# A two-layer diffusion backbone: the norm's sum of squares in two sets of matmuls

## The chip, the cores and the metric

The kernel runs on one core of a Trainium2 chip. The metric is the device time in microseconds (us) of one execution, as a median of three runs. The core's engines work side by side, each through its own queue in order: TensorE (PE in the profile; its weight loads are PEld), VectorE (DVE), ScalarE (ACT), GpSimd (POOL), and SyncE (SP), which here only issues DMAs. TensorE's clock has two levels, 1.2 and 2.4 GHz; the profile gives the granted clock as a share of the full one.

## The reference

640 tokens (128 of context, 512 latent) of width 1024 go through two layers. A layer norms x, projects it into the inputs of three mixers (differential attention, a bidirectional state-space scan, neighbourhood attention), merges their outputs, projects once more and adds the result to x. A last norm gives y. What the change touches is the norm alone:

```
def _rmsnorm(x, g):
    xf = x.astype(jnp.float32)
    y = xf * lax.rsqrt(jnp.mean(xf * xf, axis=-1, keepdims=True) + EPS)
    return (y * g.astype(jnp.float32)).astype(x.dtype)
```

## The kernel before, in words

The activations lie transposed: x is 8 tiles of 128 features by 640 tokens, worked on in two halves of 320 tokens. Nearly all matmuls are in `feat` (the matmul is line 175): an output tile of 128 features by 320 tokens takes 8 k-tiles, and each k-tile three products of high and low parts in the reduced format fp32r, 24 in all. Weights come by DMA into `raw`; ACT rounds them to `hi` (L150) and DVE makes the rest `lo` (L151).

`rms_x` (line 323) makes the norm's factor for one half. The sum over features is a sum over partitions and over the 8 tiles. ACT squares each tile (L328, L331), DVE adds the squares into `acc` (L332, seven additions), and three matmuls of one column each, with 128 tokens of `acc` as weights and a column of ones as moving data, put the sum of each token into a partition of `ms` (L338). All of this is in full fp32, and a matmul in fp32 shows as two records of the weight load and two of the matmul, so the three show as six. DVE scales and adds EPS (L339), POOL raises to the power -0.5 (L340, `r`). Then the factor must lie along the free axis again: DVE multiplies three pieces of the identity with columns of `r` (L346, `d`), and one matmul of ones with `d` (L348, `rb`, 320 columns, fp32) copies it to all partitions. The three pieces start at tokens 0, 128 and 192 of the half, so that the last repeats 64 tokens.

`rms_x` is called six times: for the two halves at the start (lines 1110 and 1113), for the two halves between the layers (through `norm`, line 1192) and for the two halves at the end (line 1194). Between the layers and at the end it follows `out_proj` (line 1051), whose eight tiles m are added to x by DVE (L1057); as each x tile comes out, its square and its addition can go. At the end DVE multiplies x by `rb` and `final_g` (L1196, eight operations per half) and SP sends each tile out. Nothing comes after the second half but this.

Who runs first on an engine is settled before the run: the program is built under a scheduler with a simulated timeline, which takes on each engine the ready instruction that comes first in the program. On the chip each engine keeps that order. `bank()` hands out PSUM tiles from a pool of three, and `warm` (line 204) shows a use that the kernel has already: matmuls that nobody reads.

Of the kernel before, what the change touches and what calls it, by code (L numbers as in the profile page):

```python
# [9 lines left out]
F32 = mybir.dt.float32  # L10
F32R = mybir.dt.float32r
AF = mybir.ActivationFunctionType
ALU = mybir.AluOpType
# [6 lines left out]
EPS = 1e-6  # L20
# [104 lines left out]
class Net:  # L125
# [106 lines left out]
    def load_first(self):  # L232
        nc, a, c = self.nc, self.a, self.const
        self.sm = {}
        self.load(["cc"])
        cc = self.sm["cc"]
        self.mhalf = c.tile([128, 8], F32, name="mhalf")
        nc.vector.memset(self.mhalf, -0.5)
        self.sc = c.tile([128, 8, 32], F32, name="sc")
        nc.vector.memset(self.sc, 0.0)  # L240
        th = c.tile([128, 8, 2], F32, name="cth")
        nc.scalar.activation(th, cc, AF.Tanh, scale=0.5)
        nc.vector.tensor_scalar(out=th, in0=th, scalar1=0.5, scalar2=0.5, op0=ALU.mult, op1=ALU.add)
        nc.vector.tensor_tensor(out=self.sc[:, :, 0:2], in0=th, in1=cc, op=ALU.mult)
# [75 lines left out]
        out.append(g)  # L320


    def rms_x(self, x, half, pool, pp):
        nc = self.nc
        h0 = half * 320
        h = slice(h0, h0 + 320)
        acc = pool.tile([128, 320], F32, tag="acc", name="acc", bufs=2)
        nc.scalar.activation(acc, x[0][:, h], AF.Square)  # L328
        for k in range(1, 8):
            sq = pool.tile([128, 320], F32, tag="sq", name="sq", bufs=2)  # L330
            nc.scalar.activation(sq, x[k][:, h], AF.Square)  # L331
            nc.vector.tensor_tensor(out=acc, in0=acc, in1=sq, op=ALU.add)  # L332
        at = (0, 128, 192)
        ps = pp.tile([128, 512], F32, tag="ms", name="ms", bufs=1)
        v = pool.tile([128, 3], F32, tag="v", name="v", bufs=2)
        r = pool.tile([128, 3], F32, tag="r", name="r", bufs=2)
        for i, c in enumerate(at):
            nc.tensor.matmul(ps[:, i:i + 1], lhsT=acc[:, c:c + 128], rhs=self.ones[:, 0:1], start=True, stop=True)  # L338
        nc.vector.tensor_scalar(out=v, in0=ps[:, 0:3], scalar1=1.0 / 1024, scalar2=EPS, op0=ALU.mult, op1=ALU.add)  # L339
        nc.gpsimd.tensor_tensor(out=r, in0=v, in1=self.mhalf[:, 0:3], op=ALU.pow)  # L340
        self.r = r
        rb = pp.tile([128, 512], F32, tag="rb", name="rb", bufs=2)[:, 0:320]
        d = pool.tile([128, 320], F32, tag="d", name="d", bufs=2)
        for i, c in enumerate(at):
            own = slice(0, 128) if i < 2 else slice(64, 128)
            nc.vector.tensor_scalar(out=d[:, c + own.start:c + 128], in0=self.ident[:, own], scalar1=r[:, i:i + 1], scalar2=None,  # L346
                                    op0=ALU.mult)
        nc.tensor.matmul(rb, lhsT=self.ones, rhs=d, start=True, stop=True)  # L348
        return rb

    def norm(self, l, x, half, ss, p, pp):
# [710 lines left out]
    def build(self):  # L1062
        nc, tc, a, o = self.nc, self.tc, self.a, self.o
        with ExitStack() as es:
# [20 lines left out]
            with self.pool("x0") as xp, self.pool("aw0", bufs=9) as wp, self.pool("ps_a0", space=PSUM) as pp:  # L1085
                xa = xp.tile([128, 8, NT], F32, name="x")
                x = [xa[:, k, :] for k in range(8)]
# [13 lines left out]
                with self.pool("norm") as np_:  # L1101
# [8 lines left out]
                    rb = [self.rms_x(x, 0, np_, pp)]  # L1110
# [22 lines left out]
            for l in range(DEPTH):  # L1133
                with ExitStack() as ph:
                    with self.pool("dv") as vp:
# [4 lines left out]
                        pp = ph.enter_context(self.pool("ps_c", space=PSUM))  # L1140
                        v = self.diff_v(l, 0, vp)
                        self.logits(l, 1, range(8))
                        self.logits(l, 0, L1)
                        with self.pool("diff") as p, self.pool("ps_d", space=PSUM) as ps:
# [3 lines left out]
                            for h in range(4):  # L1148
# [7 lines left out]
                                if h == 1:  # L1156
                                    v = self.diff_v(l, 1, vp)
                                d = self.diff_norm(att, cp, pp)
# [20 lines left out]
                with self.pool("tail") as tp, self.pool("more", bufs=3) as more, self.pool("ps_x", space=PSUM) as pp:  # L1179
                    mg = [tuple(tp.tile([128, NT], F32R, name=f"mg{s}{k}") for s in "hl") for k in range(8)]  # L1180
                    self.merges(l, 2, range(4), accd, mg=mg, spilled=range(8), more=more)
                    with self.pool("x") as xp, self.pool("norm") as np_:
                        x = [xp.tile([128, NT], F32, name=f"x{k}") for k in range(8)]
                        for k in range(8):
                            self.dma(x[k], src[k])
                        for half in range(2):
                            h = slice(half * 320, half * 320 + 320)
                            self.out_proj(l, mg, x, gate[0], half)
                            if l + 1 < DEPTH:
                                for k in range(8):  # L1190
                                    self.dma(xd[k][:, h], x[k][:, h])
                                self.norm(l + 1, x, half, nxt, np_, pp)
                            else:
                                rb = self.rms_x(x, half, np_, pp)
                                for k in range(8):
                                    nc.vector.scalar_tensor_tensor(out=x[k][:, h], in0=x[k][:, h],  # L1196
                                                                   scalar=self.sm["final_g"][:, k:k + 1], in1=rb,
                                                                   op0=ALU.mult, op1=ALU.mult)
                                    self.dma(o["y"][k][:, h], x[k][:, h])
                        src = xd  # L1200
# [25 lines left out]
```

## Time and profile before

| what | us |
|---|---|
| median of 3 runs (lowest, highest) | 1624.2 (1621.79, 1625.91) |
| the profiled execution | 1621.39 |
| its span, first to last instruction | 1619.5 |
| PE busy in the span | 1580.0 (98%) |
| DVE busy | 1069.5 (66%) |
| ACT busy | 771.9 (48%) |
| POOL busy | 159.4 (10%) |

The profiled execution is 1.89 us longer than its span, and 2.8 us below the median of the runs. Matmuls are pipelined: the duration of a record runs from its start to its modelled end, and the next may start long before that. What a row of matmuls costs is read from start to start. Mean granted clock of TensorE over the span: 0.994.

### The profile page before, as it was taken

Reading aid. Unit: us, or ns where it says so; the run is one execution under the profiler, and the core shown is the slowest. Engines: PE = TensorE matmul, PEld = TensorE weight load, DVE = VectorE, ACT = ScalarE, POOL = GpSimd, SP = SyncE. Lnnn points to the kernel's source line nnn. Section 1 sums busy time; section 2 is a strip of 40 time slices with the busy share of each in tenths; the row PEclk is TensorE's granted clock in tenths of the full one; section 3 lists DMA queues with packets and bytes.
Section 4 is the critical chain, followed back from the end, with each engine's and each line's share of the span. In section 5 each row is a group of like instructions: output and inputs, shape, how many; then the busy total and the mean of one; then the engine's idle time right before and its main releaser. Section 6 shows DMA issues by size and latency. Waiting matters only on the chain.

```text
span 1619.5 us, 29029 instructions
## 1 busy us (share of the span) xinstructions
PE 1580.0 (98%) x11311; PEld 1503.4 (93%) x11311; DVE 1069.5 (66%) x2290; ACT 771.9 (48%) x1778; POOL 159.4 (10%) x182
## 2 busy tenths in 40 slices
PE   7999999999999999999999999999999999999997
PEld 4999899999989999999989989999999899999996
DVE  5766678667546666666777667766565575577565
ACT  4545654344445454453455465434444454554332
POOL 2003412011000000000000252201010000000000
PEclk9999999999999999999999999999999999999998
DMA  9563234421233434437553222352222343344643
GB/s 338 203 249 110 94 101 145 141 73 57 85 116 104 136 111 127 150 108 250 187 174 116 86 91 89 117 189 77 67 87 80 120 130 93 111 133 152 218 156 129
DMA packets 81672, 214.62 MB, mean 133 GB/s; under 512 B 9728, under 2 KB 25664, under 8 KB 80512
## 3 DMA queue, kind: packets, MB, share of 16 engines
q1 hardware_dynamic: 80624, 211.46, 40.1%
q8 instruction: 89, 1.46, 0.4%
q0 software_dynamic: 480, 0.88, 0.1%
q10 hardware_dynamic: 432, 0.43, 0.1%
q14 instruction: 47, 0.39, 0.1%
HBM read 170.27 MB, written 34.08 MB: 126 GB/s over the span
## 4 chain that ended last, share of the span: by engine, by line
PE 88%; DMA 4%; DVE 3%; issue 2%; ACT 2%; POOL 0%; SPq 0%; POOLq 0%; DVEq 0%; ACTq 0%
PE mm L175 61%; PE mm L187 7%; PE s L959 2%; PE o L983 2%; PE o L541 2%; PE t L975 2%; PE s L526 2%; PE t L533 1%; PE g L788 1%; DMA aw<-in_w_ada 1%; PE y L801 1%; DMA raw<-in_w_feat 1%; PE y L266 1%; PE s L522 1%; DMA raw<-in_w_out 1%
## 5 line engine op out<-in xcount | busy, mean ns | idle before, releaser
L175 PE MATMUL mm<-hh,hi 128*128 128x320 f32 x1856 | 575.6, 311 | 7.0 <-ACT hh L365 2.2
L175 PE MATMUL mm<-hl,hi 128*128 128x320 f32 x1856 | 578.5, 312 | 1.7 <-DVE hl L366 1.7
L175 PE MATMUL mm<-hh,lo 128*128 128x320 f32 x1856 | 574.4, 310 | 0.7 <-DVE lo L151 0.7
L175 PEld LDWEIGHTS mm<-hh,hi 128*128 128x128 f32 x1856 | 349.0, 188 | 16.4 <-issue 3.7
L175 PEld LDWEIGHTS mm<-hl,hi 128*128 128x128 f32 x1856 | 349.0, 188 | 7.9 <-issue 2.7
L175 PEld LDWEIGHTS mm<-hh,lo 128*128 128x128 f32 x1856 | 349.5, 188 | 5.9 <-issue 3.4
L151 DVE TENSOR_TENSOR lo<-raw,hi 128x1024 fp32r<-128x1024 f32 (+2 forms) x194 | 232.6, 1200 | 94.3 <-ACT hi L150 88.6
L150 ACT ACTIVATE hi<-raw 128x1024 fp32r<-128x1024 f32 (+2 forms) x194 | 200.1, 1033 | 176.5 <-PE mm L175 120.4
L175 PE MATMUL mm<-yh,hi 128*128 128x320 f32 x384 | 118.6, 310 | 3.4 <-ACT yh L385 3.4
L175 PE MATMUL mm<-yl,hi 128*128 128x320 f32 x384 | 119.2, 310 | 0.3 <-DVE yl L386 0.2
L175 PE MATMUL mm<-yh,lo 128*128 128x320 f32 x384 | 118.1, 308 | 0.0
L187 PE MATMUL mm<-hi,hh 128*128 128x264 f32 (+1 forms) x320 | 90.7, 284 | 1.8 <-DVE vl L406 1.7
L187 PE MATMUL mm<-lo,hh 128*128 128x264 f32 (+1 forms) x320 | 91.1, 285 | 0.0
L187 PE MATMUL mm<-hi,hl 128*128 128x264 f32 (+1 forms) x320 | 90.3, 283 | 0.0
L535 ACT ACTIVATE ph<-t 128x384 fp32r<-128x384 f32 x64 | 31.4, 490 | 121.5 <-PE t L533 121.5
L175 PE MATMUL mm<-mgl,hi 128*128 128x320 f32 x256 | 78.5, 308 | 0.0
L175 PE MATMUL mm<-mgh,lo 128*128 128x320 f32 x256 | 78.0, 308 | 0.0
L175 PE MATMUL mm<-mgh,hi 128*128 128x320 f32 x256 | 77.4, 306 | 0.0
L175 PEld LDWEIGHTS mm<-yh,hi 128*128 128x128 f32 x384 | 71.9, 188 | 5.1 <-ACT yh L385 4.0
L485 DVE TENSOR_REDUCE st<-s 128x2 f32<-128x1536 f32 (+1 forms) x40 | 59.5, 1486 | 25.6 <-PE s L526 24.0
L175 PEld LDWEIGHTS mm<-yl,hi 128*128 128x128 f32 x384 | 72.1, 188 | 1.3 <-DVE yl L386 0.8
L175 PEld LDWEIGHTS mm<-yh,lo 128*128 128x128 f32 x384 | 72.1, 188 | 0.1
(311 smaller groups left out, 2908.8 us busy)
## 6 DMA issues: line engine op xcount, KB each, us to landing
raw<-in_w_feat SPq DMA_DIRECT2D x110, 512.0 KB, 3.7
aw<-in_w_ada SPq DMA_DIRECT2D x8, 2048.0 KB, 8.0
raw<-in_w_out SPq DMA_DIRECT2D x32, 512.0 KB, 3.6
thd<-th SPq DMA_DIRECT2D x48, 320.0 KB, 2.2
th<-thd SPq DMA_DIRECT2D x48, 320.0 KB, 3.7
raw<-in_w_br SPq DMA_DIRECT2D x24, 512.0 KB, 3.4
accd<-th SPq DMA_DIRECT2D x32, 320.0 KB, 2.8
ac<-accd SPq DMA_DIRECT2D x32, 320.0 KB, 3.9
```

Of the source, the lines that this page charges most:

```text
L150: nc.scalar.activation(hi, raw, AF.Copy)
L151: nc.vector.tensor_tensor(out=lo, in0=raw, in1=hi, op=ALU.subtract)
L175: nc.tensor.matmul(ps, lhsT=s, rhs=r, start=(k == 0 and n == 0), stop=(k == K - 1 and n == 2))
L187: nc.tensor.matmul(ps, lhsT=s, rhs=r, start=(k == 0 and q == 0), stop=(k == 7 and q == 2))
L266: nc.tensor.matmul(ps[32 * g:32 * g + 32, :], lhsT=self.sc[:, 4 * q + i, :], rhs=raw[:, i, 256 * g:256 * g + 256], start=(q + i == 0), sto ...
L485: nc.vector.tensor_reduce(out=st[:, 0:2], in_=s, axis=AX.X, op=ALU.max)
L526: nc.tensor.matmul(s[:, m * 768 + c0:m * 768 + c0 + 512], lhsT=q[:, qs], rhs=ks[m][:, c0:c0 + 512], start=(i == 0), stop=(i == 1))
L535: nc.scalar.activation(ph[dst], pt[:, 0:3, :], AF.Copy)
L541: nc.tensor.matmul(ov[:, 0:256], lhsT=x[:, kt, sv], rhs=q[:, kt, :], start=(kt == 0 and n == 0), stop=(kt == 5 and n == 2))
L959: nc.tensor.matmul(s[:, c0:c0 + n], lhsT=q[:, i * 128:(i + 1) * 128], rhs=ks[j][:, k0:k0 + n], start=(x == 0), stop=(x == 1))
L975: nc.tensor.transpose(pt[:, t, :], e[:, t * 128:(t + 1) * 128], self.ident)
L983: nc.tensor.matmul(out, lhsT=lw, rhs=sel(q), start=(first and x == 0), stop=(last and x == 1))
```

## The change

The eighth square is no longer added to `acc`. The three one-column matmuls are issued twice, once with `acc` (now seven tiles) into columns 0 to 2 of `ms` and once with the last square `sq` into columns 4 to 6. A DVE operation adds EPS to the first three (`v0`), another adds the second three (`v`). The factor 1/1024 moves: EPS is multiplied by 1024 and the last matmul has a tile of 32.0 (`root`, set once at the start by a DVE memset) in place of ones. The three pieces of `d` become two operations: one tensor_tensor over 256 columns with the identity and two columns of `r` both broadcast, and one tensor_scalar over 64 columns. In the last call alone (second half of the end, `keep`) two groups of matmuls without a reader are put into PE's queue: eight with the last x tile as moving data (128 columns, fp32) ahead of the second set, fourteen with `sq` as moving data behind it.

```diff
@@ load_first
+        self.root = c.tile([128, 128], F32, name="root")
+        nc.vector.memset(self.root, 32.0)
@@ rms_x
-    def rms_x(self, x, half, pool, pp):
+    def rms_x(self, x, half, pool, pp, keep=False):
...
             nc.scalar.activation(sq, x[k][:, h], AF.Square)
-            nc.vector.tensor_tensor(out=acc, in0=acc, in1=sq, op=ALU.add)
+            if k < 7:
+                nc.vector.tensor_tensor(out=acc, in0=acc, in1=sq, op=ALU.add)
         at = (0, 128, 192)
         ps = pp.tile([128, 512], F32, tag="ms", name="ms", bufs=1)
+        for j, t in enumerate((acc, sq)):
+            if keep and j == 1:
+                for _ in range(8):
+                    nc.tensor.matmul(self.bank()[:, 0:128], lhsT=self.ones, rhs=x[7][:, h0:h0 + 128], start=True, stop=True)
+            for i, c in enumerate(at):
+                nc.tensor.matmul(ps[:, 4 * j + i:4 * j + i + 1], lhsT=t[:, c:c + 128], rhs=self.ones[:, 0:1], start=True, stop=True)
+            if j == 0:
+                v0 = pool.tile([128, 3], F32, tag="v0", name="v0", bufs=2)
+                nc.vector.tensor_scalar(out=v0, in0=ps[:, 0:3], scalar1=1024 * EPS, scalar2=None, op0=ALU.add)
+        if keep:
+            for _ in range(14):
+                nc.tensor.matmul(self.bank()[:, 0:128], lhsT=self.ones, rhs=sq[:, 0:128], start=True, stop=True)
...
-        for i, c in enumerate(at):
-            nc.tensor.matmul(ps[:, i:i + 1], lhsT=acc[:, c:c + 128], rhs=self.ones[:, 0:1], start=True, stop=True)
-        nc.vector.tensor_scalar(out=v, in0=ps[:, 0:3], scalar1=1.0 / 1024, scalar2=EPS, op0=ALU.mult, op1=ALU.add)
+        nc.vector.tensor_tensor(out=v, in0=ps[:, 4:7], in1=v0, op=ALU.add)
         nc.gpsimd.tensor_tensor(out=r, in0=v, in1=self.mhalf[:, 0:3], op=ALU.pow)
...
-        for i, c in enumerate(at):
-            own = slice(0, 128) if i < 2 else slice(64, 128)
-            nc.vector.tensor_scalar(out=d[:, c + own.start:c + 128], in0=self.ident[:, own], scalar1=r[:, i:i + 1], scalar2=None,
-                                    op0=ALU.mult)
-        nc.tensor.matmul(rb, lhsT=self.ones, rhs=d, start=True, stop=True)
+        nc.vector.tensor_tensor(out=d[:, 0:256].rearrange("p (t n) -> p t n", t=2), in0=self.ident.unsqueeze(1).to_broadcast([128, 2, 128]),
+                                in1=r[:, 0:2].unsqueeze(2).to_broadcast([128, 2, 128]), op=ALU.mult)
+        nc.vector.tensor_scalar(out=d[:, 256:320], in0=self.ident[:, 64:128], scalar1=r[:, 2:3], scalar2=None, op0=ALU.mult)
+        nc.tensor.matmul(rb, lhsT=self.root, rhs=d, start=True, stop=True)
@@ build, the end
-                                rb = self.rms_x(x, half, np_, pp)
+                                rb = self.rms_x(x, half, np_, pp, keep=(half == 1))
```

## Rows read from the trace of the kernel before

**Rows 1.** The page: span and busy time, share and instructions of an engine.
```profile
span 1619.5 us, 29029 instructions
...
PE 1580.0 (98%) x11311; PEld 1503.4 (93%) x11311; DVE 1069.5 (66%) x2290; ACT 771.9 (48%) x1778; POOL 159.4 (10%) x182
```

**Rows 2.** Busy time by stretch: stretch, length, PE, PEld, DVE, ACT, POOL, clock, DMA.
```profile
790.00:800.00 10.00, 10.00 (x73) 10.00 (x72) 6.69 (x13) 4.39 (x7) 0.85 (x1) 1.00 0.73 236
...
1606.20:1608.20 2.00, 0.21 (x2) 0.00 (x0) 1.04 (x2) 0.47 (x1) 0.00 (x0) 1.00 0.00 0
...
1609.10:1610.90 1.80, 0.01 (x1) 0.01 (x1) 0.78 (x4) 0.00 (x0) 0.85 (x1) 0.71 0.00 0
1610.90:1612.40 1.50, 1.43 (x2) 0.49 (x2) 0.03 (x1) 0.00 (x0) 0.00 (x0) 0.50 0.00 0
```

**Rows 3.** Instructions in order of time, last chain: start, length, engine, line, operation, tiles.
```profile
1606.45 0.55 DVE L1057 SCALAR_TENSOR_TENSOR x<-mm,gate,x 128x320 f32<-128x320 f32 x1 [1.83 <-PE mm L175]
1607.09 0.47 ACT L331 ACTIVATE sq<-x 128x320 f32<-128x320 f32 x1 [3.00 <-DVE x L1057]
1607.59 0.49 DVE L332 TENSOR_TENSOR acc<-acc,sq 128x320 f32<-128x320 f32 x1 [0.60 <-ACT sq L331]
...
1608.23 0.80 PE L338 MATMUL ms<-masks,acc 128*128 128x1 f32 x6 [1.82 <-DVE acc L332]
1609.07 0.16 DVE L339 TENSOR_SCALAR v<-ms 128x3 f32<-128x3 f32 x1 [0.98 <-PE ms L338]
1609.31 0.85 POOL L340 TENSOR_TENSOR r<-v,mhalf 128x3 f32<-128x3 f32 x1 [24.06 <-DVE v L339]
1610.19 0.65 DVE L346 TENSOR_SCALAR d<-masks,r 128x128 f32<-128x128 f32 x3 [0.96 <-POOL r L340]
...
1610.89 1.43 PE L348 MATMUL rb<-d,masks 128*128 128x320 f32 x2 [1.86 <-DVE d L346]
1612.37 3.76 DVE L1196 SCALAR_TENSOR_TENSOR x<-x,final_g,rb 128x320 f32<-128x320 f32 x8 [1.53 <-PE rb L348]
```

**Rows 4.** PE in order of time, where the set stands among other matmuls.
```profile
796.93 0.31 PE L175 MATMUL mm<-mgh,lo 128*128 128x320 f32 x1
797.08 0.72 PE L338 MATMUL ms<-masks,acc 128*128 128x1 f32 x6
...
797.89 0.32 PE L175 MATMUL mm<-mgl,hi 128*128 128x320 f32 x1
...
1582.71 0.83 PE L338 MATMUL ms<-masks,acc 128*128 128x1 f32 x6 [0.19 <-DVE acc L332]
```

**Rows 5.** PE in order of time, between the layers, second half.
```profile
830.55 0.72 PE L338 MATMUL ms<-masks,acc 128*128 128x1 f32 x6
...
833.14 0.81 PE L348 MATMUL rb<-d,masks 128*128 128x320 f32 x2 [0.42 <-DVE d L346]
835.18 0.72 PE L175 MATMUL mm<-hh,hi 128*128 128x320 f32 x3 [1.24 <-ACT hh L365]
```

**Rows 6.** In order of time, DVE and PE at the start.
```profile
8.94 2.28 DVE L332 TENSOR_TENSOR acc<-acc,sq 128x320 f32<-128x320 f32 x4 [0.47 <-ACT sq L331]
...
11.27 0.83 PE L338 MATMUL ms<-masks,acc 128*128 128x1 f32 x6 [0.49 <-DVE acc L332]
```

**Rows 7.** PE in order of time: fp32 matmuls in a row at full clock.
```profile
153.72 0.78 PE L801 MATMUL y<-xt,ma 128*128 128x64 f32 x6
154.43 0.65 PE L742 MATMUL t<-xw,bt 128*64 128x256 f32 x4
...
1588.18 0.70 PE L348 MATMUL rb<-d,masks 128*128 128x320 f32 x2
```

**Rows 8.** Lines L348 and L757: duration in ns, least/median/most, start of first and last.
```profile
L348 PE MATMUL rb<-d,masks x12: 432/485/901, 14.0 to 1611.6; 128*128 128x320 f32 x12
...
L757 DVE TENSOR_TENSOR hs<-hs,dd x12: 409/924/1270, 147.1 to 948.4; 128x256 f32<-128x256 f32 x12
```

**Rows 9.** Busy time by stretch at the start (columns as in the second group).
```profile
12.00:14.00 2.00, 1.65 (x34) 1.01 (x34) 0.81 (x4) 0.00 (x0) 0.88 (x1) 0.61 1.02 396
```

## The prediction

> **What bounds the kernel now.** I read the page first: PE is busy for 1580.0 of 1619.5 us [rows 1]. So an instruction added to PE's queue is paid for, unless it stands where PE waits. The table by stretch says where: between the layers PE works 10.00 of 10.00 us, and after the last out-projection it works 0.21 of 2.00 us [rows 2]. The instructions in order of time then give that last chain, which nothing covers [rows 3]. It runs from the last x tile (DVE, done at 1607.00) over the square (to 1607.56), the addition (to 1608.08), the set of one-column matmuls (1608.23 to 1609.03), `v`, the power on POOL (to 1610.16), the diagonals (to 1610.84) and the `rb` matmul (1610.89 to 1612.32) to the output, which starts at 1612.37. In this chain the clock falls: 0.71 from 1609.1 on, 0.50 (1.2 GHz) under `rb` [rows 2]. `rb` takes 1.43 us there and 0.70 at full clock [rows 3, 7]. So there are 0.73 us to be had from the clock, and some 0.6 from the addition.
>
> **Prices.** A set of six one-column records among other matmuls starts at 797.08, and the second L175 record behind it at 797.89 [rows 4]; less one L175 step of 0.15 (796.93 to 797.08, the set then standing in the next one's place) the set costs PE 0.66 us.
> The matmuls without a reader are fp32, so 8 and 14 of them are 16 and 28 records. The trace has no row of such records with 128 columns. From below: the two records of `rb` take 0.70 together and one alone at least 0.43, so the second starts 0.27 after the first for 320 columns [rows 7, 8]; for 128 columns that makes 0.107. From above: 0.15, the step of L175 with 320 columns [rows 4]. The nearest row is six fp32 records of 64 columns in 154.43 - 153.72 = 0.71, that is 0.118 each [rows 7]; they are shorter, so the weight load or the issue sets their step, and ours can't be quicker than the larger of the two. I take 0.118.
>
> The Trainium skill ("TensorE: Matmul & The Clock Gate", "Part 2: What happens when you issue a matmul") says that one column of the moving operand enters per cycle. At 2.4 GHz that would be 0.053 us for 128 columns. The trace disagrees for fp32: 0.27 for 320 columns is two cycles a column. By the page's rule the second group would be over before the diagonals; that is the first rival.
>
> **The end, second half.** The first set needs seven squares only, which are in `acc` long before; it stands behind the last L175 record or among its neighbours and fits into PE's wait from 1606.2 to 1607.09 (0.66 us). If the order puts it ahead of the last tile's matmuls instead, x comes 0.66 later; I take 0. `v0` is off the chain, 0.16 as the old `v` [rows 3].
> From 1607.09, when x tile 7 is there, PE has work without a break, so the end of `rb` is a plain sum. First group 16 x 0.118 = 1.89, to 1608.98. The square was ready at 1607.56, so the second set waits 1.4 us behind the group: that is more than the addition that went away. Second set 6 x 0.118 = 0.71, to 1609.69 (results at 1609.78). Second group 28 x 0.118 = 3.30, to 1612.99. Beside it run `v` 0.16, POOL 0.85 and the diagonals, with the gaps of today: ready at 1611.55. `rb` stands behind the group, starts at 1612.99 at full clock and takes 0.70: 1613.69, against 1612.32. The end is **1.37 us later**. At 0.107 a record it is 44 x 0.011 = 0.48 less, 0.89; at 0.15 it is 44 x 0.032 = 1.41 more, 2.78.
> The diagonals are hidden here by 1.4 us of the second group. Their broadcast operation on 256 columns takes 0.409 at best and 1.270 at most in the nearest line [rows 8]; POOL is idle by then, so I take the first. With a third of today's 0.65 for the 64 columns this is 0.63: no gain. Even 1.27 would stay under the cover at the end, and would cost up to 0.84 in a call where the chain is bare.
>
> **The end, first half, and between the layers, first half.** PE is full. Each gets one more set: 0.66. At the end PE stood 0.19 for the eighth addition [rows 4], which goes. So 0.47 and 0.66. The DVE time saved (an addition of 0.49 less `v0`) buys nothing, as DVE isn't late here.
>
> **Between the layers, second half.** PE stands 0.42 before `rb` and 1.24 behind it [rows 5], so the chain counts, not only PE's work. The set that ends the chain no longer needs the addition (0.49) and can be ordered that much earlier; the added set costs 0.66 ahead of it. Together +0.2; from -0.6 (the set is absorbed in the waits and the chain comes earlier) to +0.7.
>
> **The start, both halves.** The additions come one every 0.57 us (four in 2.28), and the set follows at 11.27 for 0.83 [rows 6]. Now the first set follows the seventh square's addition, 0.6 earlier, and the second set stands behind it on PE: 0.6 saved against 0.66 added. That is 0.1 late, and later PE waits for DMA anyway. The memset of `root` lies in DVE's wait for the first input. I take 0; -0.7 if the clock, which is 0.61 from 12 to 14 us [rows 9], doesn't fall, +0.5 if both halves pay their set.
>
> **Sum.** 0.66 + 0.2 + 0.47 + 1.37 = +2.7 us: the profiled execution of 1621.39 would be 1624.1. As that execution is 2.8 below the median of the runs, I put the difference on the median: 1624.2 + 2.7 = **1626.9**. The bounds, if all come together: at best 0.7 + 0.8 + 0.48 less, +0.7; at worst 1.41 + 0.5 + 0.5 more, +5.1. The forecast's own range is 1624.9 to 1629.3. I call no change what lies within 0.3% (4.9 us).
>
> **Rivals.**
> 1. The second group doesn't hold up `rb`. Either the scheduler puts `rb` ahead of what is left of it (then `rb` ends at 1611.55 + 0.70 = 1612.25, -0.05), or a record takes half of 0.107 (first group 0.86, second set to 1608.66, diagonals at 1610.5, `rb` to 1611.2, -1.1). With 1.33 for the other calls: +0.2 to +1.3, 1624.4 to 1625.5. For it: PE's order is settled on simulated times, and the trace has `rb` both with a wait of 0.42 in front of it and without one [rows 5, 7]. Against it: the 0.27 of rows 7 and 8, and a scheduler that takes the first in program order. 0.18.
> 2. Nothing is paid: the sets go into PE's small waits, the chain between the layers is 0.5 shorter, and the end gains 1.1 as in the first. -1.6, 1622.6. Against it: 10.00 of 10.00 in rows 2. 0.12.
> 3. **Slower than the bound**: the clock falls in spite of the groups. Today it falls at about 1609.9 (0.71 over the 1.8 us from 1609.1), and at the start it fell in a stretch in which PE was busy for 1.65 of 2 us with small records [rows 2, 9]. Then what is left at 1609.9 runs at half speed: of 50 records 24 are done by then (2.81 / 0.118), and 26 x 0.214 = 5.6 and `rb` of 1.43 bring 1616.9, +4.6 at the end. With 1.33: +5.9, 1630.1. It decides at whether the rows of the end show 1.00 or 0.50 under the second group. Against it: PE hardly rests in the new chain, where it now rests for 1.8 of the 2 us from 1606.2 on [rows 2]. 0.10.
> 4. The order elsewhere shifts, as the scheduler's timeline moves by some tenths from the start on, and this outweighs the rest: to either side by more than 4.9 us. Nothing in the trace prices it. 0.08.
>
> **How the numbers follow.** The forecast has 0.52. Of it 0.03 lies above the bound with the spread of the runs. Slower: 0.10 + 0.04 + 0.03 = 0.17. Faster: half of the last rival, 0.04. Same: 0.79. The range takes in the second rival below, with the spread of a median of runs, and the third above: 1621.2 to 1630.2.
>
> **What would show it.** In the profile after: clock 1.00 under the last `rb` and 0.70 us for it; 16 and 28 records in a row, at about 0.12 each; the last `rb` starting right behind a matmul without a reader and not behind the diagonals; six more records in each of six calls, with the L175 neighbours 0.66 further apart. The last chain, from the last x tile to `rb`'s end, should be 6.7 us where it is 5.3. The prediction is wrong in its main step if `rb` waits for the diagonals, and wrong as a whole if stretches without a norm in them change their length.

## The result, and the profile after

The changed kernel takes 1633.04 us (median of 4 runs, 1631.31 to 1635.28), the kernel before on the same chip 1623.47 (4 runs, 1621.79 to 1625.91). The ratio is 1.0063, 95% interval [1.0049, 1.0077]: slower by 0.6%. The forecast was 1626.9 with a range up to 1630.2; the time lies above it. Its profiled execution took 1632.39 us, 11.0 more than the one of before.

From the page after, the span and the busy time of each engine (answers to [rows 1]):

```profile
span 1630.6 us, 29187 instructions
...
PE 1596.4 (98%) x11391; PEld 1518.2 (93%) x11391; DVE 1066.3 (65%) x2285; ACT 772.4 (47%) x1778; POOL 160.9 (10%) x182
```

PE is busy for 16.4 us more, in 80 more records, which at the 0.11 us measured below would be some 9 of it (an estimate). That says how much, not where.

**Where the time came in.** For that I matched the n-th operation of each line on DVE, ACT and POOL in the two traces and took the difference of the starts (after less before; medians). At 130 to 160 us it is -0.2. From 480 to 760 us it stands at 7.93 and does not move. At 930 to 1010 it is 9.5, at 1300 to 1450 10.7, at the end 11.1. So 8 of the 11 us came in between 160 and 480 us, in the first layer's scan and attention, where the change edits nothing. They are read from the waits.

The waits of PE in that stretch; engine, line, what it waited for, total, times, longest. Before, from 120 to 510 us:

```profile
PE mm L187 <- DVE vl L406: 1.7, 1, 1.7
...
PE s L501 <- ACT qx L436: 0.4, 1, 0.4
PE mm L175 <- DVE sh L439: 0.2, 1, 0.2
PE s L522 <- ACT e L488: 0.2, 1, 0.2
```

After, the same stretch (most lines lie 14 further on):

```profile
PE s L515 <- ACT qx L450: 2.1, 1, 2.1
PE t L547 <- DVE e L506: 2.0, 1, 2.0
PE s L536 <- ACT e L502: 1.5, 2, 1.1
PE mm L175 <- DVE sh L453: 1.0, 1, 1.0
...
PE mm L175 <- DVE st L500: 0.8, 1, 0.8
```

The wait of `s` for `qx` has grown from 0.4 to 2.1, that of L175 for `sh` from 0.2 to 1.0, that of `s` for `e` from 0.2 to 1.5; those of `t` for `e` and of L175 for `st` are new. PE's busy time, by the table of stretches (columns as in [rows 2]; the first stretch after is 8.0 us longer, as the work comes later):

Before:

```profile
150.00:500.00 350.00, 345.15 (x2370) 325.32 (x2367) 233.53 (x455) 171.00 (x404) 60.06 (x54) 1.00 0.33 104
...
240.00:260.00 20.00, 19.41 (x137) 18.97 (x136) 15.53 (x43) 7.84 (x19) 4.94 (x6) 1.00 0.35 114
```

After:

```profile
150.00:508.00 358.00, 347.39 (x2358) 324.85 (x2357) 233.43 (x455) 170.30 (x403) 64.17 (x55) 1.00 0.32 100
...
240.00:260.00 20.00, 16.86 (x107) 16.19 (x107) 15.16 (x43) 7.39 (x20) 4.95 (x6) 0.91 0.24 78
...
248.36:251.78 3.42, 3.32 (x12) 3.35 (x13) 3.10 (x13) 1.37 (x5) 2.12 (x3) 0.50 0.11 34
```

PE stands 4.85 us before and 10.61 after: 5.8 us of the 8.1 (7.93 less -0.2). The waits for `qx` and for `sh` follow each other (rows below); behind them the clock is 0.50 (1.2 GHz) for 3.42 us, which loses 1.7; before it is 1.00 throughout. 0.6 us is left that these two don't explain.

What the first wait is, by the instructions in order of time around it. Before:

```profile
236.43 0.62 ACT L823 ACTIVATE ysq<-ysb 128x512 f32<-128x512 f32 x1
...
241.61 0.60 PE L828 MATMUL t<-masks,ysb 128*128 128x128 f32 x4
...
243.51 0.89 ACT L835 ACTIVATE yh<-yf 128x128 fp32r<-128x128 f32 x4
...
244.31 0.25 ACT L436 ACTIVATE kx<-mm 128x128 f32<-128x128 f32 x1
246.18 0.28 ACT L436 ACTIVATE qx<-mm 128x128 f32<-128x128 f32 x1 [1.62 <-PE mm L175]
246.51 0.49 PE L501 MATMUL s<-kx,qx 64*128 64x128 f32 x4 [0.37 <-ACT qx L436]
```

After:

```profile
241.56 0.61 ACT L837 ACTIVATE ysq<-ysb 128x512 f32<-128x512 f32 x1
...
244.24 0.66 PE L842 MATMUL t<-masks,ysb 128*128 128x128 f32 x4
...
245.66 0.91 ACT L849 ACTIVATE yh<-yf 128x128 fp32r<-128x128 f32 x4 [3.39 <-DVE yf L844]
...
246.47 0.26 ACT L450 ACTIVATE kx<-mm 128x128 f32<-128x128 f32 x1
246.63 0.27 ACT L450 ACTIVATE qx<-mm 128x128 f32<-128x128 f32 x1
246.95 0.49 PE L515 MATMUL s<-kx,qx 64*128 64x128 f32 x4 [2.05 <-ACT qx L450]
248.46 0.61 PE L175 MATMUL mm<-hh,hi 128*128 128x320 f32 x1 [1.01 <-DVE sh L453]
```

In both kernels the way from `t` to `s` is the same: PE makes `t`, DVE `yf` from it, ACT `yh` from that, and behind `yh` in ACT's queue stand the copies `kx` and `qx` that `s` needs. What differs is what PE has to do meanwhile. Before, 27 records of L175 stand in PE's queue between `t` and `s`; at the end it is ACT that waits for PE, which has just made what `qx` copies. After, the scan's step (`ysq`) comes 5.1 us later and `s` stands right behind `t`: ACT stands 3.39 us at `yh` for DVE, and PE has nothing ahead of `s` and stands 2.05. The instructions are the same; their places in the queues are not. The other long wait, of `t` for `e` at 484 us, was not followed in this way.

Compared by line, operation, tiles and shape, PE's queue differs from that of before in some 90 places between 70 and 475 us, and in none from there to 750 us. The queues of DVE, ACT and, in a few places, POOL and SP differ in that stretch, too.

**The last chain**, in order of time, after (answers to [rows 3]):

```profile
1618.04 0.72 PE L344 MATMUL ms<-masks,acc 128*128 128x1 f32 x6
...
1618.85 1.16 PE L342 MATMUL mm<-x,masks 128*128 128x128 f32 x8
1618.89 0.47 ACT L334 ACTIVATE sq<-x 128x320 f32<-128x320 f32 x1 [3.00 <-DVE x L1071]
...
1619.84 0.73 PE L344 MATMUL ms<-masks,sq 128*128 128x1 f32 x6
...
1620.43 1.14 PE L342 MATMUL mm<-x,masks 128*128 128x128 f32 x8
...
1620.85 0.85 POOL L354 TENSOR_TENSOR r<-v,mhalf 128x3 f32<-128x3 f32 x1 [24.57 <-DVE v L353]
...
1621.40 1.50 PE L350 MATMUL mm<-sq,masks 128*128 128x128 f32 x12
1621.73 0.43 DVE L359 TENSOR_TENSOR d<-masks,r 128x256 f32<-128x256 f32 x1 [0.96 <-POOL r L354]
1622.07 0.25 DVE L361 TENSOR_SCALAR d<-masks,r 128x64 f32<-128x64 f32 x1
...
1622.74 0.70 PE L362 MATMUL rb<-d,root 128*128 128x320 f32 x2
...
1623.29 1.95 PE L350 MATMUL mm<-sq,masks 128*128 128x128 f32 x16
1623.49 1.92 DVE L1210 SCALAR_TENSOR_TENSOR x<-x,final_g,rb 128x320 f32<-128x320 f32 x4 [1.17 <-PE rb L362]
```

The scheduler split both groups: 8 of the first group's 16 records stand ahead of the second set, 12 of the second's 28 ahead of `rb` and 16 behind it. From the start of the last square to the first output operation it is 4.60 us, 5.28 before: the chain is 0.68 shorter, and `rb` runs at full clock (0.70, not 1.43).

**Between the layers**, second half, PE in order of time (answers to [rows 5]):

```profile
835.31 0.72 PE L344 MATMUL ms<-masks,acc 128*128 128x1 f32 x6
839.13 0.72 PE L344 MATMUL ms<-masks,sq 128*128 128x1 f32 x6
841.65 0.81 PE L362 MATMUL rb<-d,root 128*128 128x320 f32 x2 [0.54 <-DVE d L361]
843.70 0.72 PE L175 MATMUL mm<-hh,hi 128*128 128x320 f32 x3 [1.24 <-ACT hh L379]
```

The waits of PE are those of before within 0.12 us.

### The profile page after: what moved, and what is told of

It reads as the page before. It is cut to its first block, busy times and chain, and to the rows that moved or that the text cites. A ratio compares the mean times of both kernels' runs of the same rounds, so it can differ in the third digit from the quotient of the medians.

```text
span 1630.6 us, 29187 instructions
## 1 busy us (share of the span) xinstructions
PE 1596.4 (98%) x11391; PEld 1518.2 (93%) x11391; DVE 1066.3 (65%) x2285; ACT 772.4 (47%) x1778; POOL 160.9 (10%) x182
## 4 chain that ended last, share of the span: by engine, by line
PE 88%; DVE 5%; ACT 3%; DMA 2%; issue 1%; POOL 1%; SPq 0%; DVEq 0%; ACTq 0%; POOLq 0%
PE mm L175 62%; PE mm L187 7%; PE s L973 2%; PE o L997 2%; PE o L555 2%; PE t L989 2%; PE s L540 1%; DMA qd<-qr 1%; PE g L802 1%; PE t L547 1%; PE y L815 1%; DMA x<-in_x 1%; PE y L268 1%; ACT e L502 1%; POOL sh L454 1%
## 5 line engine op out<-in xcount | busy, mean ns | idle before, releaser
L175 PE MATMUL mm<-hh,hi 128*128 128x320 f32 x1856 | 576.4, 311 | 4.3 <-ACT vf L867 1.9
L175 PE MATMUL mm<-hl,hi 128*128 128x320 f32 x1856 | 579.2, 312 | 1.3 <-DVE hl L380 1.3
L175 PE MATMUL mm<-hh,lo 128*128 128x320 f32 x1856 | 575.2, 310 | 0.0
L175 PEld LDWEIGHTS mm<-hh,hi 128*128 128x128 f32 x1856 | 350.2, 189 | 12.3 <-ACT hh L379 3.1
L175 PEld LDWEIGHTS mm<-hl,hi 128*128 128x128 f32 x1856 | 349.6, 188 | 7.9 <-issue 3.3
L175 PEld LDWEIGHTS mm<-hh,lo 128*128 128x128 f32 x1856 | 350.0, 189 | 6.7 <-issue 4.7
L175 PE MATMUL mm<-yh,hi 128*128 128x320 f32 x384 | 119.1, 312 | 4.7 <-ACT yh L399 3.4
L175 PE MATMUL mm<-yl,hi 128*128 128x320 f32 x384 | 120.2, 313 | 0.2 <-DVE yl L400 0.2
L175 PE MATMUL mm<-yh,lo 128*128 128x320 f32 x384 | 118.7, 309 | 0.0
L175 PE MATMUL mm<-mgl,hi 128*128 128x320 f32 x256 | 78.8, 309 | 0.0
L175 PEld LDWEIGHTS mm<-yh,hi 128*128 128x128 f32 x384 | 72.3, 189 | 6.5 <-ACT yh L399 4.0
L175 PE MATMUL mm<-mgh,lo 128*128 128x320 f32 x256 | 77.9, 306 | 0.0
L175 PE MATMUL mm<-mgh,hi 128*128 128x320 f32 x256 | 77.5, 307 | 0.0
L175 PEld LDWEIGHTS mm<-yl,hi 128*128 128x128 f32 x384 | 72.7, 189 | 1.3 <-DVE yl L400 0.7
L175 PEld LDWEIGHTS mm<-yh,lo 128*128 128x128 f32 x384 | 72.7, 189 | 0.0
```

The costliest lines, as they stand in the source:

```text
L175: nc.tensor.matmul(ps, lhsT=s, rhs=r, start=(k == 0 and n == 0), stop=(k == K - 1 and n == 2))
```

## The experiments

Theories. **Order**: the edits at the start move the scheduler's simulated timeline, it writes another order for the first layer, and this order costs the 8 us. **Work**: what the changed norms do costs it directly. **Keep**: the groups without readers cost it. "Offset" below is the difference of matching starts against the profile of before, as above, at 550 to 700 us (first layer over), 930 to 1010 and the end. The kernel before ran beside each group of kernels: 1623.79 us beside e1 to e4 (23 runs), 1623.46 beside e5 to e8 (29), 1623.91 beside e9 and e10 (23). `rms_old` is the norm of before under another name. All kernels but e5 and e9 set `root` as the change does. The diffs show the lines that matter, with cuts marked.

**e1_old_start.** The two calls at the start old, the four later ones changed.

```
-  rb = [self.rms_x(x, 0, np_, pp)]
+  rb = [self.rms_old(x, 0, np_, pp)]
...
-  rb.append(self.rms_x(x, 1, np_, pp))
+  rb.append(self.rms_old(x, 1, np_, pp))
```

> The two calls at the start keep the sum and the diagonals of before; the four later calls are changed. Theory ORDER (the calls at the start make the scheduler write another order of PE's and SP's work for layer 0, and that order costs 7.9 us by 480 us of the span, where every later row stands 7.93 later): the offset in layer 0 goes to 0, what is left is +1.0 to +3.5 us over the kernel before (the sets between the layers and at the end, less 0.7 at the very end). Rival WORK (the added sets and waits of the six calls cost what they cost wherever they stand): only a third of the 11.0 us goes, +6 to +8 is left. Rival KEEP (the groups without a reader cost it): nothing goes, +10.

Measured 1623.1 us (12 runs), ratio 0.9997 [0.9987, 1.0007]; offset -1.8, 0.95, 1.9. Without the start's edit nothing of the 8 us is there, though four of the six norms are changed. By the ratio, -2.1 to +1.1 us is left, nearly all of it below the +1.0 to +3.5 expected under Order; so the timing shows no cost of the four.

**e2_only_start.** The mirror: only the two calls at the start changed.

```
-  self.norm_part(l, x, half, ss, self.rms_x(x, half, p, pp), range(8), p)
+  self.norm_part(l, x, half, ss, self.rms_old(x, half, p, pp), range(8), p)
...
-  rb = self.rms_x(x, half, np_, pp, keep=(half == 1))
+  rb = self.rms_old(x, half, np_, pp)
```

> Only the two calls at the start are changed, the four later ones are those of before. ORDER: +7 to +9 us over the kernel before, with the offset of 7.9 reached by 480 us and constant from there to 760. WORK: +2 to +4. KEEP: 0.

Measured 1633.28 us (5 runs), ratio 1.0053 [1.0041, 1.0066]; offset 9.7, 10.8, 12.0. The start alone gives the loss: the interval overlaps that of the whole change.

**e3_whole_split2.** The whole change, but the second call at the start makes the diagonals in three operations; PE's queue in the first layer is then that of before but for a few rows at the start.

```
-  nc.vector.tensor_tensor(out=d[:, 0:256]..., in0=self.ident..., in1=r[:, 0:2]..., op=ALU.mult)
-  nc.vector.tensor_scalar(out=d[:, 256:320], ...)
+  for i, c in enumerate(at):
+      nc.vector.tensor_scalar(out=d[:, c + own.start:c + 128], ...)
```

> The whole change, but for one thing: the second call at the start keeps the three diagonal operations (0.65 us in place of 0.58 on a chain); its sum is in two sets as in the change. In the queue of PE the order of layer 0 is then that of before but for the first rows. ORDER: the 7.9 us are gone though the work is the same within 0.1 us: +1 to +4 over the kernel before, and 6 to 9 below the changed kernel. WORK: within 0.5 us of the changed kernel, +9 to +11. KEEP: the same, +9 to +11.

Measured 1625.91 us (12 runs), ratio 1.0008 [0.9994, 1.0022]; offset -0.5, 3.1, 7.2. This kernel does one small operation more than the changed one, and the 8 us of the first layer are gone. In its profile PE's waits there are those of before again, 0.4 for `qx` among them, but for one of 0.8 for `th`. Its later offsets hold clock falls (below), and the timed ratio is near 1.

**e4_no_keep.** The change without the two groups.

```
-  rb = self.rms_x(x, half, np_, pp, keep=(half == 1))
+  rb = self.rms_x(x, half, np_, pp)
```

> The change without the two groups of matmuls without a reader; the order of everything ahead of the last chain is that of the changed kernel. ORDER: the changed kernel's time but for the last chain, where the clock falls again: rb takes 1.43 in place of 0.70, and the 0.6 us by which the first group held up the second set come back, so between -0.2 and +0.5 of the changed kernel, +10 to +12 over the kernel before. KEEP: -5 us or more against the changed kernel. The step of the prediction by which 28 records stand ahead of rb would give -1.4 here; the trace of the changed kernel shows rb after 12 of them.

Measured 1632.41 us (6 runs), ratio 1.0050 [1.0038, 1.0062]; offset 7.8, 9.6, 10.2. That is 6 to 10 us more than before, where Order expected 10 to 12 and Keep 5 or more below the changed kernel. Keep falls: without the groups the loss is there all the same. Its last chain, in order of time:

```profile
1617.91 0.47 ACT L334 ACTIVATE sq<-x 128x320 f32<-128x320 f32 x1 [3.00 <-DVE x L1071]
...
1618.43 0.83 PE L344 MATMUL ms<-masks,sq 128*128 128x1 f32 x6 [0.64 <-ACT sq L334]
...
1621.07 1.44 PE L362 MATMUL rb<-d,root 128*128 128x320 f32 x2 [1.81 <-DVE d L361]
1622.55 3.75 DVE L1210 SCALAR_TENSOR_TENSOR x<-x,final_g,rb 128x320 f32<-128x320 f32 x8 [1.53 <-PE rb L362]
```

It is 4.64 us from the square to the output, 4.60 with the groups: what they give back in `rb` (0.74) they take by standing ahead of the second set, which starts 0.52 behind the square's start here and 0.95 in the changed kernel, and ahead of `rb`.

**e5_tail.** Before with only the norm at the very end changed, with smaller groups (three matmuls, then six), and the old scaling, so that `root` isn't needed.

```
-  rb = self.rms_x(x, half, np_, pp)
+  rb = (self.rms_last if half == 1 else self.rms_x)(x, half, np_, pp)
```

> Only the norm at the very end is new (second half: sum of squares in two sets, diagonals in two operations, three matmuls without a reader ahead of the second set and six behind it); the norms at the start and between the layers are the old ones, and so is the queue of TensorE up to the last chain. If the time of the whole change comes from the order of the first layer (theory), the trace stands within 0.5 us of the kernel before everywhere up to 1600 us, nothing of the +7.9 us is there, and only the last chain counts: last square to the first output operation 3.9 to 4.6 us in place of 5.28, the total 0.7 to 1.4 us shorter than before (ratio 0.999). If the prediction's own step for this chain holds (work on TensorE ahead of rb pushes rb back), rb waits for the second group and the total is equal or up to 0.7 us longer. If the clock of TensorE falls in this chain all the same, the output stage costs some 3 us more.

Measured 1622.49 us (12 runs), ratio 0.9989 [0.9979, 0.9999]; offset -0.6, -0.9, 0.6. The last chain takes 4.45 us, the clock is 1.00 in it. It has the lowest ratio of this study, 0.1% under before with an interval that just leaves out 1. The offset at the end is positive in spite of it, against the expectation of 0.5 us at most up to 1600: between 1200 and 1300 us this profile's mean granted clock is 0.95, that of before 0.98. The 3 us that the expectation puts on the output stage if the clock fell are borne out by no run: the eight output operations take 3.75 us here and in e4_no_keep, where the clock under `rb` is 0.50.

**e6_second_start.** Before with only the second call at the start changed.

```
-  rb.append(self.rms_old(x, 1, np_, pp))
+  rb.append(self.rms_x(x, 1, np_, pp))
```

> Only the second of the two norms at the start is new (two sets and diagonals in two operations); everything else is the kernel before. This is the smallest edit found that still gives the changed order in the first layer's scan and attention. Order theory: +7 to +10 us against the kernel before, constant from 480 us to the layer boundary, ratio 1.0045 to 1.006. If it is the summed work of the changed norms that costs, one norm is a fifth of it and lies under the start: under +1 us.

Measured 1635.55 us (6 runs), ratio 1.0068 [1.0051, 1.0085]; offset 9.1, 10.2, 14.2. PE's waits between 120 and 510 us in its profile:

```profile
PE s L545 <- ACT qx L480: 2.1, 1, 2.1
PE t L577 <- DVE e L536: 2.0, 1, 2.0
PE s L566 <- ACT e L532: 1.5, 2, 1.2
```

One norm of six gives the same long waits as the whole change, and no smaller loss (expected under Order 1.0045 to 1.006, into which the interval reaches).

**e7_start_split_sum and e10_start_diag.** Before with one half of the edit in both calls at the start: the sum in two sets and three diagonals, or the sum in one set and two diagonals. The diff is e7's; e10 calls `rms_diag` in the same places.

```
-  rb = [self.rms_old(x, 0, np_, pp)]
+  rb = [self.rms_split(x, 0, np_, pp)]
...
-  rb.append(self.rms_old(x, 1, np_, pp))
+  rb.append(self.rms_split(x, 1, np_, pp))
```

> Both norms at the start have their sum in two sets, but keep the diagonals in three operations; everything else is the kernel before. More of the start is changed than where only its second norm is new, yet TensorE's queue in the first layer stays that of the kernel before but for a few rows. Order theory: within 0.3% of before (offset in the first layer -2 to +1 us, total -2 to +3 us). Theory that the two-set sum itself costs at the start, by its matmuls or its vector operation: +8 us as in the whole change, or more than where only one norm has it.

Measured 1624.08 us (12 runs), ratio 1.0004 [0.9995, 1.0012]; offset 1.1, 4.2, 4.2.

> Both norms at the start have their diagonals in two operations and keep the sum in one set; everything else is the kernel before, and TensorE's queue is the same but for some eight places within the start. It is the fourth corner of the square: sum split alone gave +0.04%, both together +0.5 to 0.7%. Order theory: offset within 1.5 us of before throughout the first layer, ratio 0.9990 to 1.0010. If it is the two-operation diagonal that costs (its operation with a broadcast operand), some +8 us, ratio 1.005.

Measured 1624.4 us (12 runs), ratio 1.0002 [0.9990, 1.0015]; offset -0.4, 0.8, 2.3. So neither half alone, in both calls, has a cost that the timing shows, and both halves together in one call cost 0.68% [0.51, 0.85], some 11 us (e6). A price per instruction, added up, can't do that. In both profiles `s` waits 0.4 for `qx` again, as before, and the 2.0 for `e` is gone.

**e8_root_only.** Before with the constant tile alone.

```
+  self.root = c.tile([128, 128], F32, name="root")
+  nc.vector.memset(self.root, 32.0)
```

> All norms are the old ones; a constant tile of 32 is set once on the vector engine at the start, as the change does, and nothing reads it. TensorE's queue in the first layer stays that of the kernel before; at the layer boundary some 25 places differ. Order theory: the offset is near zero up to 790 us; what it is after 840 us prices a changed order at the boundary without any norm's change, estimated 0 to +2.5 us (the whole change has +2.3 there). If the boundary's +2.3 us come from the two-set norm itself, the offset stays near zero to the end.

Measured 1623.46 us (12 runs), ratio 1.0003 [0.9992, 1.0013]; offset -0.3, 0.5, 5.1. The expectation speaks of some 25 changed places at the boundary; in this trace there are none. By line, operation, tiles and shape, every engine's queue is that of before from the first row to the last, but for the memset. So the 0.8 us that the boundary adds and the 5.1 at the end are what two executions of one order differ by: PE is at half clock for some 17 us between 520 and 1605 us here, for 3.4 in the profile of before. The gain of offset over the boundary (550 to 700 us, then 930 to 1010) is -0.3 to 3.1 us in the seven profiles whose boundary norms are the old ones, and 1.6 to 3.5 in the four that have them changed: they overlap too much for a price of the two-set norm there.

**e9_tail_after_v.** As e5_tail, with the second group (eight matmuls, not six) behind `v` and in the sets' PSUM tile; the diff is against e5_tail.

```
-  for _ in range(6):
-      nc.tensor.matmul(self.bank()[:, 0:128], lhsT=self.ones, rhs=sq[:, 0:128], ...)
...
   nc.vector.scalar_tensor_tensor(out=v, in0=ps[:, 4:7], ...)
+  for _ in range(8):
+      nc.tensor.matmul(ps[:, 0:128], lhsT=self.ones, rhs=sq[:, 0:128], ...)
```

> As the kernel in which only the norm at the very end is new, but the second group (now eight matmuls of 128 columns without a reader) stands in the program behind the operation that makes v and writes the same PSUM tile as the two sets, so that TensorE's queue holds it behind the second set. The order up to the last chain is that of the kernel before. If a record ahead of the set delays it by its 0.12 us, four records that stood ahead of the set go, and last square to first output operation is 3.9 to 4.1 us (5.28 before, 4.45 with the four records ahead); rb must still run at full clock (two records in some 0.7 us). Total 1.1 to 1.5 us under before, ratio 0.9985 to 0.9995. If the idle stretch ahead of the group lets the clock fall, rb takes 1.4 us and the gain is 0.4 us.

Measured 1623.11 us (12 runs), ratio 0.9993 [0.9982, 1.0004]. Its last chain:

```profile
1610.01 0.47 ACT L360 ACTIVATE sq<-x 128x320 f32<-128x320 f32 x1 [3.00 <-DVE x L1095]
...
1610.68 0.80 PE L370 MATMUL ms<-masks,sq 128*128 128x1 f32 x6
...
1611.73 2.05 PE L378 MATMUL ms<-sq,masks 128*128 128x128 f32 x16 [0.25 <-DVE v L376]
...
1612.98 0.25 DVE L385 TENSOR_SCALAR d<-masks,r 128x64 f32<-128x64 f32 x1
...
1613.62 0.70 PE L386 MATMUL rb<-d,masks 128*128 128x320 f32 x2
1614.36 3.76 DVE L1234 SCALAR_TENSOR_TENSOR x<-x,final_g,rb 128x320 f32<-128x320 f32 x8 [1.13 <-PE rb L386]
```

4.35 us, not the 3.9 to 4.1 expected: the set does come earlier (0.67 behind the square's start, 1.08 in e5_tail), but `rb` stands behind the group's 16 records and starts at 1613.62, when the diagonals have been ready since 1613.23. The group was too long; at 0.112 us a record, six matmuls would have ended with the diagonals (an estimate). The timing can't tell it from e5_tail.

## Why the prediction was wrong

**The step that failed** is "The start, both halves": it priced the edit there at 0 with bounds of -0.7 and +0.5, as if only its own instructions could cost. For these it may be right: at 130 to 160 us the offset is -0.2. What the edit cost was 7.8 to 9.7 us by the end of the first layer in the four profiles that have it whole in the second call, through the order. The prediction had this as its fourth rival, with 0.08 and the sentence that nothing in the trace prices it, put it at nothing in its sum, and named the sign that came true: stretches without a norm in them changed their length.

The four kernels with the new order in the first layer (the changed one, e2, e4 and e6) are 0.5 to 0.7% slower, the seven with the old one (e1, e3, e5, e7, e8, e9 and e10) lie within 0.12% of before; e3 differs from the changed kernel in one call's diagonals. Between 50 and 700 us every engine's queue is the same row for row in the four, and that of before row for row in the seven. PE stands 10.6 to 11.1 us in the four (150 to 508 us), 4.85 to 5.98 in the seven (150 to 500). That the order is the cause is shown by this; which engine's order is not, as all queues change together. That it acts by the waits and the clock fall is read from the profiles, where the four have the same three longest waits, and accounts for 7.5 of 8.1 us in the changed kernel. Why the scheduler's timeline tips just there was not traced.

Whether 0.08 was too low one case can't tell. Six forms of the start were run: two gave the new order (both calls changed; the second alone), four kept the old (the constant alone, each half of the edit alone, and the whole edit with three diagonals in the second call). That a new order is a worse one could be feared beforehand, as the old one left PE only 4.85 us of waits in 350; that is an argument, and no run shows it.

**The end, second half**: +1.37 was predicted, -0.68 measured. The clock and the prices were right: 1.00 throughout, `rb` 0.70, a record of 128 columns 0.112 in a row (twelve from 1621.40 to 1622.74; the first eight, with their start behind a wait, 0.124 each), where 0.118 was taken. By the Trainium skill ("TensorE: Matmul & The Clock Gate", "Part 2: What happens when you issue a matmul"), one column per cycle, the estimate would be 0.053; the trace disagrees. The diagonals take 0.59, where 0.63 was taken. What was wrong is the order within the chain: program order was taken for PE's order, so that all 44 records stood ahead of `rb`. The scheduler put 8 behind the second set and 16 behind `rb`. That is the first rival, held at 0.18: the scheduler puts `rb` ahead of what is left of the group. Its bounds for this place (-0.05 to -1.1) hold the measured value, but in part by luck: its price for this way was -0.05, as it left the first group whole ahead of the second set, and the -1.1 came from records at half price, which the 0.112 refutes. Rival 3, the clock falling in spite of the groups, fell; e4_no_keep shows what it was about, 1.44 for `rb` where PE rests.

**Price of a set**: right. In the changed kernel a set starts at 801.54 and the second L175 record behind it at 802.36; less one step of 0.145 this is 0.68, predicted 0.66.

**Between the layers**: +0.86 predicted. The offset rises by 1.6, and a clock fall at 845.7 to 849.1, which the profile of before doesn't have, can make 1.7 of it; with the old norms the rise is -0.3 to 3.1 (e8 above). The term is neither confirmed nor refuted. The same holds for +0.47 at the end's first half. From the first layer to the end the offset grows by 3.2 us; the changed kernel has three stretches at half clock between 520 and 1605 us, before has one, and the two more lose 3.4 us of full matmul work. So nothing of these 3 us need be the norms'.

**Rival 2**, nothing is paid, is near what the later four calls did: e1_old_start has them all at 0.9997 [0.9987, 1.0007], where the prediction's sum for them was +2.7 us (0.17%). That sum was too high mainly by the 2.05 us at the end (1.37 and 0.68); the 0.65 left lies within the interval.

## What to carry to other kernels

Where a scheduler with a simulated timeline writes the queues, an edit near the start can have two prices: its own instructions, and the chance that what stands behind it is reordered. Compare the queues before and after the edit stretch by stretch; where they differ in a stretch that you didn't touch, look there first, and try neighbouring forms of the edit (three diagonals for two, here) to get the old order back. Make an edit that pays at the end (0.7 us of the last chain here) at the end only. Before you trust an offset of one profile, run a kernel of the same order a second time (e8 here) and see what it differs by.

Matmuls that only hold the clock must stand where they delay nothing on the chain: ahead of the set and ahead of `rb` they took back the 0.74 us that they gave.

## What the runs showed that was not expected

Without any change of order the clock falls in other places from profile to profile. Between 1200 and 1300 us the mean granted clock is 0.98 in before, 0.95 in e5_tail and 0.97 in e8_root_only, which have one order there, and 0.98 in the changed kernel and 1.00 in e4_no_keep, which have another. One such fall, as that of 248.36 to 251.78 us, costs up to 1.7 us of full matmul work, and by the end e8_root_only is 5.1 us behind before with the same queues. So small offsets of a single profile in the second layer are worth little, and the timed ratios decide; by the end of the first layer the seven kernels with the old order lie within -1.8 to 1.1 us, the four with the new one at 7.8 to 9.7.

An fp32 record takes 0.112 us from start to start in a row of its kind at full clock, with 128 columns (twelve from 1621.40) as with 64 (from 153.89 in the trace of before) and with one (from 1619.87): here the columns don't count. Two records of `rb` with 320 columns are 0.27 apart (1622.74 and 1623.02). The 0.118 of the prediction is the same row of 64 columns with its ends in it [rows 7].
